# GLA gates beside the values in 512 columns, and results turned by VectorE and by stores

## The chip, the core and the metric

The kernel runs on one core of one Trainium2 chip (the other cores idle). The metric is the time of one execution on the device in microseconds (us); of several runs the median is given. Everything is fp32 on the outside; the large products run in fp32r, split in two parts.

## What is computed

One step of a hybrid decoder layer, for a prompt of 2048 tokens and for 8 samples that each add one token to a state. The width is 1024. Cut to what matters:

```
hn  = rmsnorm(x) * (1 + scale) + shift           # shift, scale, gate = silu(c) @ w_ada + b_ada
xa, za, q, k, v, glr, zg = split(hn @ w_in)      # 1024, 1024, 512, 512, 1024, 16, 1024 columns

# RG-LRU group: 8 blocks of 128 channels
xc    = conv4(xa);  gx, ga = sigmoid(xc @ w_gate + b)
h     = scan(a(ga) * h + sqrt(1 - a^2) * gx * xc);   y_lru = h * silu(za)

# GLA group: 4 heads, keys of 128, values of 256
S_t   = diag(alpha_t) S_(t-1) + k_t^T v_t;  o_t = q_t S_t
y_gla = o * rsqrt(mean(o*o) + eps) * g_gla_norm * silu(zg)

y     = rmsnorm(x + gate * (concat(y_lru, y_gla) @ w_out))
```

The last states of the convolution, of the LRU and of GLA, for the prompt and for the samples, are outputs too.

## The kernel before

**Products.** Each factor is split into a high and a low part, and a product is three matmuls: high by high, high by low, low by high. The normalized input stands in `hh` and `hl`, feature by token. The prompt goes in two halves of 1024 tokens (`TH`); a half is cut in segments (`SEGS`): 512 and 512 in half 0; 384, 384 and 264 in half 1, where the last holds 256 tokens and the 8 samples. TensorE's accumulators are four PSUM banks (`acc`, L53), two banks for transposes (`tps`, L56), one for the state update (`kv`) and one for the GLA output (`o`).

**Weights.** `weights` (L261) brings a piece of `w_in`. In half 0 the raw piece (512 KB) is loaded, split by ACT (L281) and VectorE (L282), and the parts (1 MB) are stored (L301); in half 1 the parts are loaded back (L284). The split weights have three buffers, the raw ones two. SyncE (SP) issues all loads and most stores in order.

**Projections.** `project` (L615) holds weights still and streams a segment's tokens (L621 to L623): the result is channel by token. It gives XA, ZA, K, Q and the GLA gates ZG. `values` (L734) streams weights past a 128-token tile instead (`value_mm`, L314, L317 to L319, 24 matmuls of 256 columns a tile): token by channel, as GLA wants its values. In half 1 `sample_values` (L710) gives the 8 samples' values with raw fp32 weights (L718), in four column groups side by side.

**Order.** The program is written in TensorE's order. `after(units, fn)` (L645) puts a step on a heap by a clock that `tick` (L649) advances with each unit of projection; so the work of GLA chunks, LRU gates and outputs is put between projections. Each head is followed by LRU tiles: heads in the order 3, 0, 1, 2 (`HEADS`), LRU tiles (0), (1, 2), (3, 4), (5, 6, 7) behind them (`LRU_TILES`), in each half. `ada_gate` (L665) computes the final gate from `w_ada` in four steps that each load 1 MB, under the first LRU tile.

**A GLA head** (`gla_head`, L937): values; keys and queries by segment with their decays (`gla_decay`, `gla_qk`); then, chunk by chunk of 128 tokens, state and output (`gla_chunk`, L847; L856 to L864 on TensorE, S updated at L865 and L866, the output copied to `on` at L869, its squares summed by ACT at L148). `gla_norm` (L872) takes the rsqrt (twelve small VectorE instructions, L125) and scales `on` by it (L877). The head's gates are projected channel by token, 128 channels at a time, and `silu2` (L915) forms z(1 + tanh(z/2)) with ACT (L919) and VectorE (L920). `gla_out` (L923) turns `on` by TensorE transposes (L929; in the last segment a small matmul, L931, puts the samples behind), multiplies by g_gla_norm (`gsc`) and the gate on VectorE (L934), and `spill` (L630) stores 128 channels by the segment's tokens to `mixd` in DRAM by ACT's queue (L635). The samples' state and output are `sample_state` (L879) and `sample_out` (L897).

**An LRU tile** (`lru_units`, L1010): XA by segment, convolution on VectorE (L1027), gate matmuls in three parts (L1053 to L1055), and a chain of ACT and VectorE over the whole half (L1056 to L1068: multiplications, square root, scan), then ZA with its silu, and the product (L1084), spilled as above.

**Tail.** `load_mix` (L1202) loads 128 tokens of all 16 channel tiles from `mixd` and splits them; `split_wo` (L1233) splits w_out; `mm3` (L1325) does the output projection, `Out` the gate, the residual and the last norm. It begins under the last LRU tiles of half 1.

## Time and profile before

| what | value |
|---|---|
| median of 3 runs | 1497.78 us (1495.71 to 1497.83) |
| the profiled execution | 1496.99 us |
| its span, first to last instruction | 1495.2 us |
| TensorE busy | 1474.0 us, 8973 matmul records |
| VectorE busy | 846.1 us, 2139 instructions |
| ACT busy | 594.7 us, 1058 instructions |
| granted TensorE clock, mean | 0.997 |

The span is what the trace covers; 1.8 us of the execution lie around it. PE is TensorE, PEld its weight loads (which overlap the matmuls), DVE is VectorE, POOL GpSimd, SP SyncE. A row of a grouped view names line, engine, operation, output<-inputs, shape, count, then busy us and mean ns of one, then the engine's idle time just before and what ended it. Matmuls are pipelined, so that the length of one is longer than its distance from the next.

### The profile page before, as it was taken

The numbers are of one execution on the slowest core, as the hardware profiler recorded it, in microseconds if no ns is written. First come the engines' busy times: TensorE is split into PE (matmuls) and PEld (weight loads), VectorE is DVE, ScalarE is ACT, GpSimd is POOL, SyncE is SP. The second block draws the span as 40 slices with busy tenths as digits, with TensorE's granted clock in tenths as the row PEclk, the third lists the DMA queues.
The fourth block names the chain that finished last, engine by engine and source line by source line (L and its number), as shares of the span: only waits on it lengthen the run. The fifth ranks groups of instructions, "written<-read, shape, count | busy, mean of one in ns | idle before, by whom it ended". The sixth has DMA issues, their size and how long they took to land.

```text
span 1495.2 us, 22861 instructions
## 1 busy us (share of the span) xinstructions
PE 1474.0 (99%) x8973; PEld 1306.9 (87%) x8973; DVE 846.1 (57%) x2139; ACT 594.7 (40%) x1058; POOL 92.9 (6%) x117
## 2 busy tenths in 40 slices
...
GB/s 324 256 152 169 222 124 166 158 161 107 165 152 139 219 122 127 141 117 149 141 110 113 163 96 134 132 83 168 179 99 229 171 113 85 113 111 64 108 43 29
DMA packets 141681, 211.30 MB, mean 141 GB/s; under 512 B 7427, under 2 KB 102563, under 8 KB 140926
## 3 DMA queue, kind: packets, MB, share of 16 engines
...
q10 hardware_dynamic: 32048, 16.00, 3.6%
...
## 4 chain that ended last, share of the span: by engine, by line
PE 52%; DVE 2%; ACT 2%; DMA 1%; issue 0%; POOL 0%; ACTq 0%; DVEq 0%
PE acc L1328 7%; PE acc L1329 7%; PE acc L1330 7%; PE acc L621 7%; PE acc L622 7%; PE acc L623 7%; PE acc L317 1%; PE acc L318 1%; PE acc L319 1%; PE po L864 1%; PE tp L929 1%; PE tp L830 0%; DMA raw<-in_w_out_dram 0%; PE acc L1053 0%; DMA w<-parts 0%
## 5 line engine op out<-in xcount | busy, mean ns | idle before, releaser
L621 PE MATMUL acc<-hh,w 128*128 128x384 f32 (+2 forms) x1256 | 445.7, 355 | 0.5 <-DMA w<-parts 0.4
L622 PE MATMUL acc<-hl,w 128*128 128x384 f32 (+2 forms) x1256 | 435.5, 347 | 0.0
L623 PE MATMUL acc<-hh,w 128*128 128x384 f32 (+2 forms) x1256 | 434.0, 346 | 0.0
L621 PEld LDWEIGHTS acc<-hh,w 128*128 128x128 f32 x1256 | 236.0, 188 | 23.1 <-issue 3.2
L623 PEld LDWEIGHTS acc<-hh,w 128*128 128x128 f32 x1256 | 235.9, 188 | 19.6
L622 PEld LDWEIGHTS acc<-hl,w 128*128 128x128 f32 x1256 | 236.1, 188 | 19.3 <-issue 0.4
L1329 PE MATMUL acc<-wol,mh 128*128 128x512 f32 (+1 forms) x528 | 202.3, 383 | 1.3 <-DVE wol L1236 1.3
L1328 PE MATMUL acc<-woh,mh 128*128 128x512 f32 (+1 forms) x528 | 203.0, 384 | 0.0
L1330 PE MATMUL acc<-woh,ml 128*128 128x512 f32 (+1 forms) x528 | 202.1, 383 | 0.0
L317 PE MATMUL acc<-w,hh 128*128 128x256 f32 (+1 forms) x508 | 145.1, 286 | 0.3 <-POOL hh L182 0.2
L319 PE MATMUL acc<-w,hl 128*128 128x256 f32 (+1 forms) x508 | 143.5, 282 | 0.2 <-DVE hl L206 0.2
L318 PE MATMUL acc<-w,hh 128*128 128x256 f32 (+1 forms) x508 | 143.2, 282 | 0.0
L1351 DVE TENSOR_TENSOR r<-acc,gbc 128x512 f32<-128x512 f32 (+1 forms) x33 | 22.3, 675 | 190.1 <-PE acc L1330 179.5
L1328 PEld LDWEIGHTS acc<-woh,mh 128*128 128x128 f32 x528 | 99.2, 188 | 26.1 <-issue 6.9
L1329 PEld LDWEIGHTS acc<-wol,mh 128*128 128x128 f32 x528 | 99.2, 188 | 21.1 <-DVE wol L1236 2.2
L1330 PEld LDWEIGHTS acc<-woh,ml 128*128 128x128 f32 x528 | 99.2, 188 | 19.4
L919 ACT ACTIVATE zs<-acc 128x512 f32<-128x512 f32 (+2 forms) x80 | 41.1, 513 | 179.5 <-PE acc L623 179.4
L920 DVE SCALAR_TENSOR_TENSOR zs<-zs,acc 128x512 f32<-128x512 f32 (+2 forms) x80 | 46.3, 578 | 91.3 <-ACT zs L919 91.3
L317 PEld LDWEIGHTS acc<-w,hh 128*128 128x128 f32 x508 | 96.1, 189 | 2.1 <-DVE vl L748 0.4
L319 PEld LDWEIGHTS acc<-w,hl 128*128 128x128 f32 x508 | 96.0, 189 | 0.4 <-DVE hl L206 0.4
L318 PEld LDWEIGHTS acc<-w,hh 128*128 128x128 f32 x508 | 95.5, 188 | 0.2
L1027 DVE SCALAR_TENSOR_TENSOR cv<-xa,vecT,cv 128x384 f32<-128x384 f32 (+2 forms) x120 | 76.9, 650 | 29.8 <-POOL cv L1025 29.5
...
## 6 DMA issues: line engine op xcount, KB each, us to landing
...
```

Source lines behind the costliest of these rows:

```text
L317: PE.matmul(ps, hh[:, kt, c], hi[:, kt % 4], start=kt == 0, stop=False)
L318: PE.matmul(ps, hh[:, kt, c], lo[:, kt % 4], start=False, stop=False)
L319: PE.matmul(ps, hl[:, kt, c], hi[:, kt % 4], start=False, stop=kt == KT - 1)
L621: PE.matmul(ps[:, :n], hi[:, kt], a, start=kt == 0, stop=False)
L622: PE.matmul(ps[:, :n], hi[:, kt], b, start=False, stop=False)
L623: PE.matmul(ps[:, :n], lo[:, kt], a, start=False, stop=kt == KT - 1)
L919: S.activation(z, ps, AF.Tanh, scale=0.5)
L920: V.scalar_tensor_tensor(z, z, 1.0, ps, op0=OP.add, op1=OP.mult)
L1027: V.scalar_tensor_tensor(cv[:, cq], xa[:, cq.start + k:cq.stop + k], cw[k], cv[:, cq], op0=OP.mult, op1=OP.add)
L1328: PE.matmul(ps, mh[:, q], woh[k][:, c], start=first, stop=False)
L1329: PE.matmul(ps, mh[:, q], wol[k][:, c], start=False, stop=False)
L1330: PE.matmul(ps, ml[:, q], woh[k][:, c], start=False, stop=last)
```

## The change

- For heads 0, 1 and 2, in each half, a new class `Pairs` projects the values and the gates together, token by channel: 256 columns of V and 256 of ZG side by side, 512 to a matmul, four 128-token tiles at a time in the four `acc` banks. `group(0)` (tiles 0 to 3) stands before the last LRU tile of the head before, `group(1)` (tiles 4 to 7) after it. The weights come in four quarters of two k-tiles (1 MB of parts each): the first has a buffer of its own, the other three take the three buffers, and are loaded for each group. The weights of K and Q are asked for inside group 1, Q's after step (2, 3), the last but one of its 16.
- While a group runs, the LRU gate matmuls use the transpose banks. Before `group(0)`, what is left of `ada_gate` is emitted (`flush_kind(4)`); `ada_gate` begins inside the first head, and its steps follow each other after 1.5 units instead of 3.
- Head 3 keeps `values`; its gates are projected token by channel as well, eight tiles with 256 columns.
- The gates' silu is formed per 128-token tile (`gate_out`), stored to DRAM (`zd`) and brought back a segment at a time into one buffer `zl` (`gate_back`).
- `gla_norm` only forms rs. `gla_out` multiplies `on` by rs and the gate, turns each 32x32 block on VectorE into `zl`, and four stores a segment (ACT's queue) put the blocks where they belong in `yd`, in runs of 32 elements. `g_gla_norm` is folded into the split of w_out. A segment's chunks after the first wait, in emission, for `gla_out` of the segment before.
- The samples' gates come with their values in half 1: four sample parts in each `group(0)` (raw fp32 weights, 128 columns in each of four column groups, through a transpose bank, added up in `zr` by VectorE), for head 3 in `sample_gates`; `turn_gates` turns them by small matmuls; `gla_out_samples` writes the samples' results. `sample_out` uses a transpose bank instead of `o`.
- In the tail `load_mix` loads a token tile in six pieces instead of four.

Counted in the two programs, TensorE's matmuls are: of 512 columns token by channel 0 before and 1152 after, of 256 columns (V) 1152 and 384; of `project`, 512 wide 1464 and 1080, 384 wide 1536 and 1152, 264 wide 768 and 576; transposes of `on` 128 and 0; sample matmuls of 64 columns 96 and 0, of 128 columns 0 and 112; eight small ones for the samples' gates are new.

```diff
+LAST = (6, 7)
...
-    mixd = dpool.tile([16, P, 16, P], F32, tag="mixd", name="mixd")
+    mixd = dpool.tile([16, P, 8, P], F32, tag="mixd", name="mixd")
+    yd = dpool.tile([H, 16, 2, P, P], F32, tag="yd", name="yd")
+    zd = dpool.tile([H, 16, P, DV], F32, tag="zd", name="zd")
...
+    def flush_kind(n):
+        while any(e[n] for e in pend):
+            e = min(e for e in pend if e[n])
             pend.remove(e)
             heapq.heapify(pend)
+            clock[0] = max(clock[0], e[0])
             e[2]()
+
+    def flush_gla():
+        flush_kind(3)
...
-            after(3, mm)
+            after(1.5, mm, bank=True)
...
     def gla_norm(nch, run):
-        _, on, ss = run
-        rs = gp.tile([P, 4], F32, tag="ors", name="ors")
+        ss = run[2]
+        rs = gp.tile([P, 4], F32, tag="ors", name="ors", bufs=2)
         rsqrt(gp, rs[:, :nch], ss[:, :nch], nch, P, 1.0 / DV)
-        for c in range(nch):
-            V.tensor_scalar(on[:, c], on[:, c], rs[:, c:c + 1], None, op0=OP.mult)
+        return rs
...
-        po = psum.tile([P, 512], F32, tag="o", name="po", bufs=1)[:, :DV]
+        po = tps()[:, :DV]
...
-    def gla_out(half, h, s, on, os_, zs):
+    gated_rows, back, side_by_side = set(), [None], [False]
+    def gate_out(h, tt, ps, z):
+        S.activation(z, ps, AF.Tanh, scale=0.5)
+        V.scalar_tensor_tensor(z, z, 1.0, ps, op0=OP.add, op1=OP.mult)
+    def gate_store(half, h, tt, z):
+        t = half * 8 + tt
+        S.dma_start(zd[h, t:t + 2].rearrange("t p c -> p t c"), z.rearrange("p (t c) -> p t c", c=DV))
+        gated_rows.update((h, t + n) for n in range(2))
+    def gate_back(half, h, s):
         c0, n = SEGS[half][s]
-        nch = min(n, TH - c0) // P
-        for dt in range(2):
-            pt = tps()
-            for c in range(nch):
-                PE.transpose(pt[:, c * P:(c + 1) * P], on[:, c, dt * P:(dt + 1) * P], ident)
-            if os_ is not None:
-                PE.matmul(pt[:, nch * P:n], os_[:, dt * P:(dt + 1) * P], sel4, start=True, stop=True)
-            ct = 2 * h + dt
-            z = zs[dt]
-            V.scalar_tensor_tensor(z, pt[:, :n], gsc[:, ct:ct + 1], z, op0=OP.mult, op1=OP.mult)
-            spill(z, 8 + ct, half, c0, n)
-
-    def gla_head(half, h, wv=None):
+        t0, nch = half * 8 + c0 // P, min(n, TH - c0) // P
+        if back[0] or any((h, t) not in gated_rows for t in range(t0, t0 + nch)):
+            return None
+        back[0] = h, half, s
+        z = yp.tile([P, 4, DV], F32, tag="zl", name="zl")
+        SP.dma_start(z[:, :nch], zd[h, t0:t0 + nch].rearrange("t p c -> p t c"))
+        return z
+    def pair_raw(h, q):
+        raw = wp.tile([P, 1088], F32, tag="wr", name="wr")[:, :1024].rearrange("p (k n) -> p k n", n=512)
+        for n, col in enumerate((V0 + h * DV, ZG + h * DV)):
+            SP.dma_start(raw[:, :, n * DV:(n + 1) * DV], i["w_in"][
+                0, 2 * q * P:(2 * q + 2) * P, col:col + DV].rearrange("(k p) n -> p k n", p=P))
+        return raw
+    def pair_weights(h, q):
+        both = (yp.tile([P, 2, 1088], F32R, tag="wy", name="w") if q == 0 else
+                wp.tile([P, 2, 1088], F32R, tag="w", name="w", bufs=3))
+        c = slice(48, 48 + 1024)
+        hi, lo = [both[:, j, c].rearrange("p (k n) -> p k n", n=512) for j in range(2)]
+        if ("vz", h, q) in parts:
+            SP.dma_start(both[:, :, c].bitcast(F32), parts["vz", h, q])
+            return hi, lo
+        raw = pair_raw(h, q)
+        S.copy(hi, raw)
+        V.tensor_tensor(lo, raw, hi.bitcast(F32), op=OP.subtract)
+        parts["vz", h, q] = dpool.tile([P, 2, 1024], F32, tag=f"vz{h}_{q}", name="parts")
+        SP.dma_start(parts["vz", h, q], both[:, :, c].bitcast(F32))
+        return hi, lo
+    class Pairs:
+        def __init__(self, half, h):
+            self.half, self.h, self.w, self.zs = half, h, [None], []
+            self.v, self.wkq = ([], []), []
+        def group(self, g):
+            half, h, w = self.half, self.h, self.w
+            if g == 0:
+                flush_kind(4)
+            w[1:] = [pair_weights(h, q) for q in range(1, 4)]
+            for x, tag in zip(self.v, ("vh", "vl")):
+                x.append(gp.tile([P, 4, DV], F32R, tag=tag, name=tag, bufs=2))
+            vh, vl = [x[g] for x in self.v]
+            side_by_side[0] = True
+            ps = [acc() for _ in range(4)]
+            samples = g == 0 and half == 1
+            raws = [pair_raw(h, q) for q in range(2)] if samples else []
+            for q, j in [(q, j) for q in (0, 1) for j in range(4)] + [(q, j) for j in range(4) for q in (2, 3)]:
+                hi, lo = w[q]
+                tt = 4 * g + j
+                c = slice(tt * P, (tt + 1) * P)
+                for k in range(2):
+                    kt = 2 * q + k
+                    PE.matmul(ps[j], hh[:, kt, c], hi[:, k], start=kt == 0, stop=False)
+                    PE.matmul(ps[j], hh[:, kt, c], lo[:, k], start=False, stop=False)
+                    PE.matmul(ps[j], hl[:, kt, c], hi[:, k], start=False, stop=kt == KT - 1)
+                if q == 3:
+                    S.copy(vh[:, j], ps[j][:, :DV])
+                    V.tensor_tensor(vl[:, j], ps[j][:, :DV], vh[:, j].bitcast(F32), op=OP.subtract)
+                    if j % 2 == 0:
+                        z = lp.tile([P, 512], F32, tag="zs", name="zs", bufs=4)
+                    gate_out(h, tt, ps[j][:, DV:], z[:, j % 2 * DV:(j % 2 + 1) * DV])
+                    if j % 2:
+                        after(0.25, lambda tt=tt, z=z: gate_store(half, h, tt - 1, z), True)
+                tick(0.25)
+                if g == 1 and (q, j) in ((1, 3), (2, 3)):
+                    self.wkq.append(weights((0, K0, Q0)[q] + h * DK, DK))
+                if samples and (q, j) in ((0, 3), (1, 3), (2, 0), (3, 1)):
+                    sample_part(q, raws[q])
+                    if q < 2:
+                        raws.append(pair_raw(h, q + 2))
+            side_by_side[0] = False
+            if samples:
+                for n in range(2):
+                    SP.dma_start(vsd[h][:, n * P:(n + 1) * P], zr[32 * n:32 * n + NS])
+                after(1, lambda: turn_gates([ident[:, 64 + 32 * n:64 + 32 * n + NS] for n in range(2)], self.zs), True)
+    def sample_part(q, raw):
+        ps = tps()[:, :P]
+        for k in range(2):
+            for g in range(4):
+                PE.matmul(ps[32 * g:32 * g + NS], fs[:, 2 * q + k], raw[:, k, g * P:(g + 1) * P],
+                          start=k == 0, stop=k == 1)
+        for g in range(4):
+            r = slice(32 * g, 32 * g + NS)
+            if q == 0:
+                (S.copy if g % 2 else V.tensor_copy)(zr[r], ps[r])
+            else:
+                V.tensor_tensor(zr[r], zr[r], ps[r], op=OP.add)
+    def turn_gates(sels, zs):
+        pt = tps()[:, :2 * NS]
+        for n in range(2):
+            PE.matmul(pt[:, n * NS:(n + 1) * NS], zr, sels[n], start=True, stop=True)
+        z = yp.tile([P, 2 * NS], F32, tag="zq", name="zq")
+        S.activation(z, pt, AF.Tanh, scale=0.5)
+        V.scalar_tensor_tensor(z, z, 1.0, pt, op0=OP.add, op1=OP.mult)
+        zs.append(z)
+    def sample_gates(w, zs):
+        ps = acc()[:, :P]
+        for m in range(0, KT, 2):
+            for g in range(4):
+                kt = m + g // 2
+                c = g % 2 * P
+                PE.matmul(ps[32 * g:32 * g + NS], fs[:, kt], w[kt // 4][2][:, kt % 4, c:c + P],
+                          start=m == 0, stop=m == KT - 2)
+        for g in range(4):
+            r = slice(32 * g, 32 * g + NS)
+            (S.copy if g % 2 else V.tensor_copy)(zr[r], ps[r])
+        after(1, lambda: turn_gates([sel2[:, n] for n in range(2)], zs), True)
+    def gla_out(half, h, s, on, rs, z):
+        t0, nch = SEGS[half][s][0] // P, min(SEGS[half][s][1], TH - SEGS[half][s][0]) // P
+        for c in range(nch):
+            V.scalar_tensor_tensor(on[:, c], on[:, c], rs[:, c:c + 1], z[:, c], op0=OP.mult, op1=OP.mult)
+        for c in range(nch):
+            V.transpose(z[:, c], on[:, c])
+        def store():
+            back[0] = None
+            y = z[:, :nch].rearrange("p c (a i) -> p (c a) i", i=32)
+            for b in range(4):
+                S.dma_start(dram(yd, (h * 16 + half * 8 + t0) * 2 * P * P + 32 * b,
+                                 [[P, 32], [32 * P, nch * 8], [1, 32]]), y[32 * b:32 * b + 32])
+        after(1, store, True)
+    def gla_out_samples(h, os_, z):
+        pt = tps()[:, :2 * NS]
+        for n in range(2):
+            PE.matmul(pt[:, n * NS:(n + 1) * NS], os_[:, n * P:(n + 1) * P], sel4, start=True, stop=True)
+        for n in range(2):
+            ct = 2 * h + n
+            c = slice(n * NS, (n + 1) * NS)
+            V.scalar_tensor_tensor(mixs[:, 8 + ct], pt[:, c], gsc[:, ct:ct + 1], z[:, c], op0=OP.mult, op1=OP.mult)
...
+            if c == 1:
+                if rows_busy[0]:
+                    after(0.5, lambda: chunks(s, c), True)
+                    return
+                rows_busy[0] = True
+            if c == 2:
+                zl[s] = gate_back(half, h, s)
...
-        wz = [weights(ZG + (2 * h + dt) * P, P) for dt in range(2)]
-        for s in range(ns):
-            c0, n = SEGS[half][s]
-            for dt in range(2):
-                zs[s, dt] = silu2(wz[dt], c0, n)
-                tick()
+            ada_gate()
+        if pairs:
+            return
+        wz = row_weights(ZG + h * DV, DV, half == 1)
+        if half == 1:
+            sample_gates(wz, sgs)
+        for tt in range(8):
+            if tt % 2 == 0:
+                z = lp.tile([P, 512], F32, tag="zs", name="zs", bufs=4)
+            ps = acc()[:, :DV]
+            value_mm(ps, slice(tt * P, (tt + 1) * P), wz, DV, (0, KT))
+            gate_out(h, tt, ps, z[:, tt % 2 * DV:(tt % 2 + 1) * DV])
+            if tt % 2:
+                after(0.5, lambda tt=tt, z=z: gate_store(half, h, tt - 1, z), True)
+            tick(0.75 if half else 0.5)
...
+                    ps = (tps() if side_by_side[0] else acc())[:, :sn]
...
+                after(2 if half == 0 and j in (0, 5, 6) else 3, lambda: gates(t, [s]))
...
+    for half in range(2):
+        pairs = None
+        for k, h in enumerate(HEADS):
+            gla_head(half, h, None if half or k else wv0, pairs)
+            js = LRU_TILES[k]
+            if k == 3:
+                lru(1, js[:-len(LAST)]) if half else lru_last_a(js)
+                break
+            pairs = Pairs(half, HEADS[k + 1])
+            pairs.w[0] = pair_weights(HEADS[k + 1], 0)
+            lru(half, js[:-1])
+            pairs.group(0)
+            lru(half, js[-1:])
+            pairs.group(1)
     flush_gla()
+    ypx.close()
...
+                dst, k = mr[-1][:, p[0][0] - q:p[0][0] - q + n], p[0][1]
+                if k < 8:
+                    (G if tt < 2 and k in LAST else SP).dma_start(dst, mixd[tt, :, k:k + n])
+                else:
+                    SP.dma_start(dst, yd[(k - 8) // 2, tt, k % 2:k % 2 + n].rearrange("k p t -> p k t"))
...
+            g = gsc[:, k - 8:k - 7]
+            S.activation(woh[k], raws[k], AF.Copy, scale=g)
+            V.scalar_tensor_tensor(wol[k], raws[k], g, woh[k].bitcast(F32), op0=OP.mult, op1=OP.subtract)
```

87 lines of the change are left out of this document (44 added, 43 removed).

## The prediction

> **What bounds the kernel now.** I read the page first: its span, the busy times, the chain that ended last.
>
> ```profile
> span 1495.2 us, 22861 instructions
> PE 1474.0 (99%) x8973; PEld 1306.9 (87%) x8973; DVE 846.1 (57%) x2139; ACT 594.7 (40%) x1058; POOL 92.9 (6%) x117
> ...
> PE 52%; DVE 2%; ACT 2%; DMA 1%; issue 0%; POOL 0%; ACTq 0%; DVEq 0%
> ```
>
> TensorE is busy 99% of the span, and where the chain is named it is TensorE's by far. The profiled execution took 1496.99 us, 1.8 us more than its span and 0.8 under the median of the runs shown (1497.78). I forecast against 1496.99.
>
> The table by stage tells whether this holds where the change works. Four of its rows, from the second half of the prompt:
>
> ```profile
> 600.00:700.00 100.00, 99.46 (x740) 96.61 (x739) 63.16 (x206) 40.09 (x81) 6.15 (x11) 1.00 0.43 139
> 700.00:800.00 100.00, 99.87 (x690) 97.23 (x690) 58.28 (x201) 35.78 (x77) 6.44 (x11) 1.00 0.36 121
> 800.00:900.00 100.00, 99.48 (x745) 97.45 (x744) 55.78 (x152) 44.39 (x79) 7.43 (x7) 1.00 0.39 127
> 900.00:1000.00 100.00, 100.00 (x757) 98.47 (x757) 60.38 (x172) 43.14 (x78) 7.37 (x10) 1.00 0.38 128
> ```
>
> Columns: stretch, its length, then PE, PEld, DVE, ACT, POOL busy (instructions), granted clock, DMA share, GB/s. The clock is 1.00, VectorE has some 40% free on average, the DMA engines 60%. So TensorE's own time is what counts, and any new wait of TensorE adds whole.
>
> A matmul's printed duration is no price, since matmuls overlap. The pace is, from start to start over undisturbed runs. Four stretches of TensorE's timeline give it, by first row and first row after:
>
> ```profile
> 257.12 0.39 PE L621 MATMUL acc<-hh,w 128*128 128x512 f32 x1
> ...
> 273.44 0.39 PE L1053 MATMUL acc<-xh,wg 128*128 128x512 f32 x1
> ...
> 281.60 0.28 PE L317 MATMUL acc<-w,hh 128*128 128x256 f32 x1
> ...
> 304.21 0.40 PE L761 MATMUL acc<-gls,g2s 128*128 128x512 f32 x1
> ...
> 931.97 0.28 PE L621 MATMUL acc<-hh,w 128*128 128x264 f32 x1
> ...
> 935.57 0.34 PE L621 MATMUL acc<-hh,w 128*128 128x384 f32 x1
> ...
> 946.78 0.33 PE L621 MATMUL acc<-hh,w 128*128 128x384 f32 x1
> ...
> 957.18 0.28 PE L621 MATMUL acc<-hh,w 128*128 128x264 f32 x1
> ```
>
> They hold 72, 192, 30 and 60 matmuls, so one of 512 columns takes 16.32/72 = 0.2267 us, of 256 22.61/192 = 0.1178, of 264 3.60/30 = 0.1200, of 384 10.40/60 = 0.1733. Two rows of the page matter too (busy us, mean ns of one | idle before it, and what ended that):
>
> ```profile
> L317 PE MATMUL acc<-w,hh 128*128 128x256 f32 (+1 forms) x508 | 145.1, 286 | 0.3 <-POOL hh L182 0.2
> ...
> L317 PEld LDWEIGHTS acc<-w,hh 128*128 128x128 f32 x508 | 96.1, 189 | 2.1 <-DVE vl L748 0.4
> ```
>
> A weight load lasts 189 ns, yet matmuls 117.8 ns apart follow without gaps: loads overlap, and a 256-wide matmul isn't bound by them.
>
> **The change part by part.** *Pairing* (heads 0, 1, 2). In half 0 a head's values are 192 matmuls of 256 and its gates 96 of 512: 192 x 0.1178 + 96 x 0.2267 = 44.4 us. In half 1 the gates are 96 of 384 and 48 of 264: 22.6 + 16.6 + 5.8 = 45.0. Paired, both are 192 of 512 = 43.5 us. That is -0.85 and -1.5 a head, three heads: -7.0. Head 3's gates turn from 96 x 512 (21.8) and 96 x 384 + 48 x 264 (22.4) into 192 x 256 (22.6) each: +1.0. Together **-6.0 us**. The evictions stay off the path; they split one 512-wide pair into two 256-wide.
>
> The Trainium skill, "TensorE: Matmul & The Clock Gate", section "Wait — 56ns, not 53.3ns?", has a warm gap of N/2.4 ns + 2.5: 109 ns for 256 and 216 for 512. The trace's 117.8 and 226.7 differ; by the rule the pairing, worked out the same way, would give -2.1 instead of -6.0, and the forecast below would be 3.9 us later. The measurement decides.
>
> *Turning* the results by TensorE goes: 128 transposes. The chain shows six of them, a grouped row the count, and the line's own view what it waited for:
>
> ```profile
> 669.24 0.66 PE tp L929 x6
> ```
> ```profile
> L929 PE MATMUL tp<-ident,on 128*128 128x128 f32 x128 | 19.0, 277 | 0.0
> ```
> ```profile
>   DVE on L877: 0.7, 3
>   issue: 0.2, 1
> ```
>
> 128 x 0.66/6 = **-14.1 us**, and 0.9 us of waits: **-0.9**. What replaces it stands on VectorE, ACT's queue and the DMA engines, off the path as long as TensorE never waits for it; the results are read back only in the tail, hundreds of us later for the early heads.
>
> *Samples.* The gates of the 8 samples no longer ride in the 264-wide matmuls; they come with the values, in fp32, 128 columns by four. 24 sets of four at 64 columns go, 28 sets at 128 come. The nearest rows, from the chain and from the timeline:
>
> ```profile
> 689.01 1.01 PE acc L718 x64
> ```
> ```profile
> 137.88 1.07 PE L677 MATMUL acc<-xt,sc 128*32 128x256 f32 x16
> 138.88 0.50 PE L1053 MATMUL acc<-xh,wg 128*128 128x512 f32 x1
> ```
>
> One set leaves eight records: 64 columns cost 1.01/8 = 0.126 us, 256 columns 1.00/2 = 0.50. For 128 I take the value in proportion, 0.25: 28 x 0.25 - 24 x 0.126 = **+4.0 us** (+0.5 if it cost no more than 64 columns, +11 if as much as 256). Eight small matmuls turn these gates; the similar L931 lasts 216 ns:
>
> ```profile
> L931 PE MATMUL tp<-sel,os 128*128 128x8 f32 x16 | 2.3, 216 | 0.0
> ```
>
> Between nothing and 8 x 0.216 = 1.7 I take half, **+0.9**. TensorE's own work: -6.0 - 14.1 - 0.9 + 4.0 + 0.9 = **-16.1 us**.
>
> **New waits.** (a) A group holds all four banks that projections use, so LRU gates and samples go through the two transpose banks, each of which VectorE or ACT must empty first. In half 1 the four sample parts of group(0) add sixteen small evictions. VectorE's queue then holds, ahead of them, the LRU tile's chain:
>
> ```profile
> L869 DVE COPY on<-po 128x256 f32<-128x256 f32 x64 | 26.7, 417 | 0.0
> ...
> L748 DVE TENSOR_TENSOR vl<-acc,vh 128x256 fp32r<-128x256 f32 x56 | 23.6, 421 | 53.1 <-ACT vh L747 52.9
> ...
> L877 DVE TENSOR_SCALAR on<-on,ors 128x256 f32<-128x256 f32 x64 | 18.6, 350 | 0.6
> ...
> L1068 DVE TENSOR_TENSOR_SCAN tg<-xl,hc,tx 128x1024 f32<-128x1024 f32 x6 | 14.3, 2384 | 0.0
> ...
> L1064 DVE SCALAR_TENSOR_TENSOR tx<-tx,cv 128x1032 f32<-128x1032 f32 x8 | 9.9, 1233 | 6.7 <-ACT tx L1056 6.6
> ...
> L1066 DVE TENSOR_TENSOR tx<-tx,tg 128x1032 f32<-128x1032 f32 x8 | 9.8, 1226 | 0.0
> ...
> L1084 DVE SCALAR_TENSOR_TENSOR zs<-tg,zs 128x384 f32<-128x384 f32 x16 | 8.7, 549 | 0.0
> ...
> L1065 DVE SCALAR_TENSOR_TENSOR tg<-xl,tg 128x1032 f32<-128x1032 f32 x6 | 7.4, 1233 | 18.3 <-ACT tg L1063 18.3
> ...
> L1084 DVE SCALAR_TENSOR_TENSOR zs<-tg,zs 128x264 f32<-128x264 f32 x8 | 3.4, 426 | 0.1
> ```
>
> The chain, L1064 to L1084, is 1.23 + 1.23 + 1.23 + 2.38 + 0.55 + 0.55 + 0.43 = 7.6 us. Also in a sample group of about 24 us (21.8 of matmuls, 2 of samples) come four evictions of values and gates (8 x 0.42 = 3.4), chunk work (two chunks of three passes, some 2.4), three multiplications by rs and gate (1.3), three block transposes (unseen; between L877's 0.35 and twice that, 1.1 to 2.1), the rsqrt's small steps and the sample additions (some 24 at 0.15 to 0.2, about 4). Together 20 to 21 us of 24: VectorE goes from 60% to over 80%, and what is queued behind the chain comes late. TensorE waits for nothing at best, for the whole 7.6 us a head at worst. Since two banks give slack, I take a fifth, 1.5 us a head, three heads: **+4.5** (0 to 22.8).
>
> (b) ada_gate's matmuls move under the first group, and each step issues two 512 KB loads for the next. One step follows its predecessor by some 20 matmuls of 512, 4.6 us. A load of the same 1 MB is in the chain:
>
> ```profile
> 846.67 5.97 DMA w<-parts
> ```
>
> 5.97 - 4.6 = 1.4 us late; I take **+1.0** (0 to 4.2, three such steps).
>
> (c) The Q weights are asked for behind 15 of group 1's 16 steps, 15 x 6 x 0.2267 = 20.4 us in. K's first segment is done at 21.8 + 24 x 0.1733 = 25.9 us. 5.5 us for a load of 5.97: 0.5 us late, three heads, **+1.5** (0 to 3). The value weights of the groups have 12 us and more. In half 0 K's segment is wider, and nothing is late.
>
> Sum of waits +7.0; -16.1 + 7.0 = -9.1: 1496.99 - 9.1 = **1487.9, say 1488 us**.
>
> **The rivals.**
> 1. *No new wait*: the queues have slack, as the averages by stage (56 to 63% of VectorE) say. 1496.99 - 16.1 = 1481. Against it: the averages hide a chain of 7.6 us in one piece. Chance 0.20.
> 2. *Slower: VectorE's queue in the sample groups*. TensorE waits for a sample's bank while the LRU chain runs, in three groups. From 13.6/3 = 4.5 us a head on (16.1 less the 2.5 of b and c) the gain is gone; with the whole chain, 22.8 + 2.5 - 16.1 = +9.2: 1506. For it: 20 of 24 us filled, and evictions whose order the program fixes. Against it: two banks, and chains that need not start right there. Chance 0.17.
> 3. *Stores in 128-byte pieces*. The turned results leave in 32-element runs, 2 M elements / 32 = 65,536 pieces. The nearest row is ACT's queue before, in 512-byte packets:
>
> ```profile
> q10 hardware_dynamic: 32048, 16.00, 3.6%
> ```
>
> 3.6% of 16 x 1495.2 us over 32048 is 27 ns a packet. At that price the pieces take 65,536/16 x 27 ns = 110 us of each engine, 0.07 of the span on top of 0.36 to 0.43: room enough. But a segment of three chunks leaves in four stores of 32 x 24 pieces; these 3072 take 3072/16 x 27 ns = 5.2 us of all 16 engines, and where they meet the Q load, they stretch it. With half of that in each head of half 1 it is 3.1 us late instead of 0.5, three heads +9.3: waits of 14.8, 1495.7, no change. Chance 0.12, with other sums of small waits of that size. The Trainium skill, "DMA: Bandwidth & Descriptors", section "Specifications", speaks for this one: under 512 B a transfer misses line rate, since the engine reads, modifies and writes. No run here shows such pieces; were each twice as long, the share would rise by 0.15, and the Q load would be 5.7 us late.
> 4. *Pairing saves much*: by printed durations, 192 x (2 x 281 - 389) ns would be 33 us for each half-head. The paces refute it. Chance 0.01.
>
> That the change doesn't do what it says, I rule out for TensorE's count: the transposes are gone from its program, 1152 matmuls of 512 columns stand for the pairs.
>
> **How the numbers follow.** Forecast 1488 (1484 to 1493, with waits between 3 and 12 us): 0.50. Rival 1: 0.20; rival 2: 0.17; rival 3: 0.12; rival 4: 0.01. The bound for "same" is 0.2%, 3 us, about what a measurement of this kernel can tell: faster is under 1494.8. So faster 0.50 + 0.20 + 0.01 = 0.71, same 0.12, slower 0.17. Unknown sizes: samples +0.5 to +11 (-3.5 to +7 on the sum), waits 0 to 30. The range leaves out the upper part of rival 2 and rival 4: 1480 to 1500.
>
> **What the profile after would show.** The paired lines at a pace of 227 ns and no L929's like; sample sets at 0.25 us; under TensorE's waits, DVE's evictions of the sample banks at three places in half 1, of 1 to 2 us each, ahead of all others; the Q load under 1 us each. I am wrong if fp32 sets of 128 columns cost 0.5 us, if the block transposes take over 0.7 us each, or if the projections' four banks make TensorE wait between groups, in half 0 too, for the evictions of the group before.

## The result, and the profile after

| | median | runs | ratio to before, 95% interval |
|---|---|---|---|
| before | 1497.80 us (1495.71 to 1497.87) | 4 | |
| changed | 1510.68 us (1507.84 to 1511.32) | 4 | 1.0086 [1.0068, 1.0103] |

The change makes the kernel 12.9 us slower. 1488 was forecast, with 1480 to 1500 as the range: it is outside, and on the other side of no change.

The page of the changed kernel, the same three lines as before:

```profile
span 1509.0 us, 21924 instructions
...
PE 1475.7 (98%) x8317; PEld 1267.1 (84%) x8317; DVE 870.1 (58%) x2230; ACT 599.4 (40%) x1088; POOL 80.3 (5%) x117
...
PE 49%; DVE 6%; ACT 3%; issue 2%; DMA 1%; POOL 1%; ACTq 0%; DVEq 0%; POOLq 0%
```

656 matmul records are gone, yet TensorE's busy time is 1.7 us higher and the span 13.8 us longer; in the chain that ended last, VectorE has risen from 2% to 6%. The table by stage shows two different things. First the four stretches that the prediction shows, then two others, and those two in the kernel before:

```profile
600.00:700.00 100.00, 98.57 (x734) 89.50 (x733) 58.55 (x194) 33.17 (x74) 4.92 (x9) 1.00 0.58 185
700.00:800.00 100.00, 99.86 (x605) 94.07 (x604) 61.77 (x183) 42.65 (x85) 7.84 (x13) 1.00 0.51 158
800.00:900.00 100.00, 99.80 (x598) 88.47 (x597) 58.76 (x169) 42.13 (x77) 2.49 (x3) 1.00 0.56 178
900.00:1000.00 100.00, 99.67 (x650) 90.62 (x650) 65.97 (x210) 37.80 (x79) 8.47 (x14) 1.00 0.56 176
...
500.00:600.00 100.00, 93.04 (x551) 78.94 (x550) 73.90 (x177) 59.20 (x101) 16.79 (x20) 0.97 0.50 158
1100.00:1200.00 100.00, 92.86 (x482) 71.17 (x482) 64.31 (x105) 53.32 (x73) 8.88 (x11) 0.98 0.52 162
```
```profile
500.00:600.00 100.00, 98.39 (x612) 84.94 (x611) 74.00 (x164) 61.57 (x101) 18.46 (x21) 1.00 0.45 147
1100.00:1200.00 100.00, 97.65 (x491) 75.37 (x490) 64.55 (x108) 46.09 (x68) 6.33 (x8) 1.00 0.49 160
```

In the middle of half 1, where the groups with samples stand, TensorE is as full as before: the wait that the forecast feared most, and rival 2's, isn't there. Where half 0 ends (500 to 600) and where half 1 runs out (1100 to 1200), TensorE loses about 5 us of 100 each that it did not lose before, and its clock falls.

The pace of the paired matmuls: first row of a group, the next, and the first row behind its 96.

```profile
721.27 0.40 PE L1014 MATMUL acc<-w,hh 128*128 128x512 f32 x1
721.51 0.40 PE L1015 MATMUL acc<-w,hh 128*128 128x512 f32 x1
...
743.66 0.34 PE L779 MATMUL acc<-gls,g2s 128*128 128x384 f32 x1
```

22.39 us / 96 = 0.2332 us, not 0.2267. The new waits of TensorE, the five longest (us in total, times, longest):

```profile
PE tp L183 <- ACT hnf L186: 3.0, 3, 2.1
PE acc L1247 <- ACT xh L1234: 2.9, 2, 2.7
PE acc L1247 <- DVE zs L937: 2.5, 1, 2.5
PE acc L695 <- DMA xt<-in_w_ada_dram: 2.2, 1, 2.2
PE acc L1247 <- ACT xa L1312: 2.1, 1, 2.1
```

L183 is `modulate`, the transposes of the next half's input at the end of half 0; L1247 is the first of the LRU gate matmuls; L695 is `ada_gate`. All but L695's are LRU work and the half's end, and none of these was foretold at its place; `ada_gate`'s wait was.

**Where the 13.8 us came from.** I added up the distances from one matmul's start to the next by the program's function, so that a wait counts to the matmul before it. In us, before, after and difference:

| function | before | after | |
|---|---|---|---|
| pairs (`group`), `project`, `value_mm` | 906.8 | 908.4 | +1.6 |
| `gla_out`, and `gla_out_samples` behind it | 15.0 | 2.2 | -12.8 |
| samples' values and gates (`sample_part`, `sample_gates`, the 64-column sets) | 3.0 | 7.6 | +4.6 |
| `turn_gates` | 0 | 1.5 | +1.5 |
| `modulate` | 5.9 | 11.1 | +5.2 |
| `gla_chunk` | 64.8 | 68.8 | +4.1 |
| LRU `gates` | 47.8 | 51.6 | +3.8 |
| `state_outputs` | 0.9 | 3.8 | +2.9 |
| `sample_values`, its 68-column matmuls | 1.4 | 4.2 | +2.8 |
| all others | | | 0.0 |

The first four lines are TensorE's own work: -5.1 against a forecast of -16.1. The rest, +18.9 against +7.0, is waits and the slower clock behind some of them (the 2.2 us of L695 stand under `gla_chunk`); by the page, TensorE's idle time alone rose by 12.1 us, from 21.2 to 33.3 of the span. The two differences, 11.0 and 11.9, are the miss of 22.9.

**The stall at 530 us, step by step.** It is the longest. The timelines of ACT and then VectorE in the changed kernel (start, length, instruction, and in brackets the idle time before it and what ended that):

```profile
514.07 1.06 ACT L1257 ACTIVATE tg<-tg 128x1024 f32<-128x1024 f32 x1
```
```profile
511.35 0.34 DVE L884 TENSOR_SCALAR S<-S,f 128x256 f32<-128x256 f32 x1
517.32 0.42 DVE L883 TENSOR_TENSOR S<-S,pkv 128x256 f32<-128x256 f32 x1 [5.62 <-PE po L882]
...
523.96 0.42 DVE L883 TENSOR_TENSOR S<-S,pkv 128x256 f32<-128x256 f32 x1 [5.63 <-PE po L882]
...
524.96 1.21 DVE L1259 SCALAR_TENSOR_TENSOR tg<-xl,tg 128x1024 f32<-128x1024 f32 x1
...
528.00 2.28 DVE L1262 TENSOR_TENSOR_SCAN tg<-xl,tx 128x1024 f32<-128x1024 f32 x1
```

VectorE idles 5.6 us twice, each time until TensorE reaches a GLA chunk whose state it must update (L883). L1259, the next step of the LRU chain, multiplies what ACT's L1257 had ready at 515.13. It runs at 524.96, since it stands behind both chunks in VectorE's queue, and for 7.8 of these 9.8 us VectorE does nothing (515.13 to 517.32, and 5.63). So the scan runs from 528.0, most of the next tile's convolution behind it, and TensorE, which needs that convolution, stops:

```profile
529.25 1.04 PE L183 MATMUL tp<-ident,xt 128*128 128x128 f32 x8
532.96 1.22 PE L1247 MATMUL acc<-xh,wg 128*128 128x512 f32 x2 [2.68 <-ACT xh L1234]
533.98 0.63 PE L633 MATMUL acc<-hh,w 128*128 128x512 f32 x1
534.41 0.63 PE L634 MATMUL acc<-hl,w 128*128 128x512 f32 x1
...
536.35 0.40 PE L1248 MATMUL acc<-xl,wg 128*128 128x512 f32 x1
536.59 0.40 PE L1249 MATMUL acc<-xh,wg 128*128 128x512 f32 x1
```

Two things are to be seen: 2.68 us of idle time, and behind it matmuls of 512 columns 0.43 us apart (533.98 to 534.41) until 536.1, then 0.24. The granted clock says the same, as the eighth column:

```profile
530.00:535.00 5.00, 2.32 (x8) 1.72 (x7) 5.00 (x12) 0.66 (x2) 0.00 (x0) 0.77 0.35 105
535.00:540.00 5.00, 5.00 (x21) 4.04 (x20) 4.68 (x10) 1.79 (x3) 0.00 (x0) 0.89 0.28 114
```

The clock was halved for some 3.2 us of work, which costs 1.6 beside the stall. It fell like that behind the waits at 530, 567 and 1100 us, and not behind those at 125 and 1122. So 4 to 5 of the 18.9 us are clock.

Why only three of the five? The clock's records change on a fixed grid of 3.41 us. The waits at 530, 567 and 1100 put 2.42, 2.36 and 2.16 us of idle time into one such window, and the window after it ran at half the clock; those at 125 and 1122 lie across a border, with 1.15 and 1.06, and 1.13 and 1.35 us. In the traces of all twenty kernels, from 40 us on, each of the 58 windows at full clock with 1.85 us of idle time or more was followed by one at half, none of the 8438 with less than 1.67 was, and of the ten between four were.

**The other stalls.** The one at 1100 is of the same kind. VectorE's queue stands before the product by the gates, which are still on their way back from DRAM (`zl`), and the steps of the next tile's convolution behind it wait too:

```profile
1098.48 0.88 DVE L1083 SCALAR_TENSOR_TENSOR on<-on,ors,zl 128x256 f32<-128x256 f32 x2 [2.09 <-DMA zl<-zd]
...
1099.96 0.52 DVE L1235 TENSOR_TENSOR xl<-cv,xh 128x384 fp32r<-128x384 f32 x1
```

L1235's input was ready at 1096.47 (ACT's L1234). The convolution ends late, ACT's cast of it stands ahead of the copy that frees TensorE's bank (L1312, at 1102.75), and TensorE waits until 1103.28. Ahead of the stall at 1122, though, VectorE is busy for 16.1 of the 17 us from 1108 to 1125; load isn't ruled out there. That at 567 was not followed back to its start.

### The profile page after: what moved, and what is told of

Read it like the earlier page. It is cut to its first block, busy times and chain, and to the rows that moved or that the text cites. A ratio compares the mean times of both kernels' runs of the same rounds, so it can differ in the third digit from the quotient of the medians.

```text
span 1509.0 us, 21924 instructions
## 1 busy us (share of the span) xinstructions
PE 1475.7 (98%) x8317; PEld 1267.1 (84%) x8317; DVE 870.1 (58%) x2230; ACT 599.4 (40%) x1088; POOL 80.3 (5%) x117
## 3 DMA queue, kind: packets, MB, share of 16 engines
q10 hardware_dynamic: 90544, 24.39, 6.9%
q8 instruction: 65, 1.06, 0.3%
## 4 chain that ended last, share of the span: by engine, by line
PE 49%; DVE 6%; ACT 3%; issue 2%; DMA 1%; POOL 1%; ACTq 0%; DVEq 0%; POOLq 0%
PE acc L1537 7%; PE acc L1538 7%; PE acc L1539 7%; PE acc L633 4%; PE acc L635 4%; PE acc L634 4%; PE acc L1014 3%; PE acc L1016 2%; PE acc L1015 2%; PE acc L325 1%; PE acc L327 1%; PE acc L326 1%; DVE tg L1262 1%; PE po L882 1%; DMA mr<-mixd 1%
## 5 line engine op out<-in xcount | busy, mean ns | idle before, releaser
L633 PE MATMUL acc<-hh,w 128*128 128x384 f32 (+2 forms) x936 | 330.7, 353 | 0.2 <-ACT tg L1250 0.2
L634 PE MATMUL acc<-hl,w 128*128 128x384 f32 (+2 forms) x936 | 323.8, 346 | 0.0
L635 PE MATMUL acc<-hh,w 128*128 128x384 f32 (+2 forms) x936 | 323.6, 346 | 0.0
L634 PEld LDWEIGHTS acc<-hl,w 128*128 128x128 f32 x936 | 176.1, 188 | 15.5 <-issue 0.9
L633 PEld LDWEIGHTS acc<-hh,w 128*128 128x128 f32 x936 | 176.1, 188 | 15.1 <-ACT tg L1250 0.4
L635 PEld LDWEIGHTS acc<-hh,w 128*128 128x128 f32 x936 | 175.9, 188 | 14.6
L1014 PE MATMUL acc<-w,hh 128*128 128x512 f32 x384 | 155.4, 405 | 0.0
L1016 PE MATMUL acc<-w,hl 128*128 128x512 f32 x384 | 151.7, 395 | 0.0
L1015 PE MATMUL acc<-w,hh 128*128 128x512 f32 x384 | 151.6, 395 | 0.0
L1221 DVE SCALAR_TENSOR_TENSOR cv<-xa,vecT,cv 128x512 f32<-128x512 f32 (+2 forms) x120 | 77.1, 644 | 23.1 <-POOL cv L1219 22.1
L1014 PEld LDWEIGHTS acc<-w,hh 128*128 128x128 f32 x384 | 72.1, 188 | 19.4 <-issue 3.2
L1015 PEld LDWEIGHTS acc<-w,hh 128*128 128x128 f32 x384 | 72.1, 188 | 16.4
L1418 ACT CAST mh<-mr 128x256 fp32r<-128x256 f32 (+2 forms) x48 | 34.8, 759 | 111.6 <-PE acc L1538 106.2
L325 PE MATMUL acc<-w,hh 128*128 128x256 f32 (+1 forms) x252 | 73.4, 291 | 0.1
```

What stands on the lines that cost most here:

```text
L325: PE.matmul(ps, hh[:, kt, c], hi[:, kt % 4], start=kt == 0, stop=False)
L633: PE.matmul(ps[:, :n], hi[:, kt], a, start=kt == 0, stop=False)
L634: PE.matmul(ps[:, :n], hi[:, kt], b, start=False, stop=False)
L635: PE.matmul(ps[:, :n], lo[:, kt], a, start=False, stop=kt == KT - 1)
L1014: PE.matmul(ps[j], hh[:, kt, c], hi[:, k], start=kt == 0, stop=False)
L1015: PE.matmul(ps[j], hh[:, kt, c], lo[:, k], start=False, stop=False)
```

## The experiments

Theories at the outset: **(1)** the pace of 512-wide matmuls depends on the byte place of the streamed weights, and the pairs' weights stand at an unfavourable one; **(2)** the stalls at the ends of the halves come since the last head's gates were moved ahead, so that less projection stands over its chunks and the last LRU chains. Rivals: the pace is the pairs' own, and VectorE's added work (multiplying and turning) makes the stalls. Theories that came up later are told by the expectations themselves. Each run's time is beside a before of 1496.8 to 1497.7 us on the same chip.

**The pace.** The weights of each head and half at another offset; then all of them at good ones.

```diff
-        c = slice(48, 48 + 1024)
+        off = 16 if q == 0 else 0        # e5; e1: another for each head and half
+        c = slice(off, off + 1024)
```

> Each head's and half's paired weights stand at another place in their buffers, so that the moving operand lies 0, 32, 64, 96, 128 or 224 bytes off the stationary activations within 256 bytes (192 and 128 in the changed kernel). Theory 1 (the pace hangs on where the two operands stand to each other): the paired matmuls of head 0 in half 0, at the same place, go at 226.7 ns, the others at 233.3; that is 192 x 6.6 ns = 1.3 us, so the time is 1507 to 1511. Rival (with the activations stationary and weights moving, 512 columns always take 233.3): all six runs of matmuls at 233.3 ns, no difference between heads.

1508.77 us, one run. Undisturbed pace by the place that the edit gives the weights' first byte, in bytes from the start of their buffer (the first quarter, in a buffer of its own, 64 bytes further): 226.8 ns at 0, 229.2 at 64, 232.5 at 128, and 233.2 to 233.4 at 32, 96, 224 and (the changed kernel) 192. Theory 1 holds.

> The changed kernel with the paired weights put at the place within 256 bytes where the activations stand (offset 0, and 16 elements in the first quarter's own buffer). Theory 1, as the run with several offsets showed it: all paired matmuls at 226.7 ns instead of 233.3, 1152 x 6.6 ns = -7.6 us: 1501 to 1505. Rival (the stalls at the halves' ends take the gain back, since VectorE sets the end there): 1507 to 1511.

1506.35 us, 1.0063 [1.0050, 1.0075]: 4.3 us under the changed kernel. The pairs fell from 273.4 to 268.7 us. One run of 48 matmuls in it:

```profile
176.51 0.39 PE L1015 MATMUL acc<-w,hh 128*128 128x512 f32 x1
...
187.39 0.39 PE L1015 MATMUL acc<-w,hh 128*128 128x512 f32 x1
```

10.88/48 = 0.2267. So the pace that I forecast was to be had, but over all 1152 it is 268.7/1152 = 0.2332 us even here: other work breaks in at 41 places, mostly for 0.1 to 0.2 us each, 6.3 us in all (4.9 at 37 places in the changed kernel), and some stretches run at 230 to 235 ns, 1.3 us. So of the 7.5 us that the place costs in the changed kernel, 1152 x 6.5 ns, 4.7 came back.

Does the place matter in the kernel before, at 256 columns?

```diff
-        q = 48 if n == DV else 0
+        q = 0                            # e12; e13: another for each head and half
```

> The kernel before the change, with the value weights (256 columns) at offset 0 instead of 48 elements, so that they stand where the activations stand within 256 bytes. Theory 1 for 256 columns too: all of them at 113.3 ns rather than mostly 117.8, 1152 x 3.7 ns = -4 us: 1492 to 1495. Rival (the rule holds for 512 columns alone): 117 to 120 ns, 1496 to 1500.

1500.63 us, 1.0026 [1.0016, 1.0035], slower: at 0 a matmul of 256 takes 119.8 to 120.0 ns in all six stretches of heads 0, 1 and 2. At 192 bytes, in the kernel before, heads 1 and 2 have 117.8, but head 0 114.6 in half 0 and 113.4 in half 1:

```profile
690.29 0.28 PE L319 MATMUL acc<-w,hl 128*128 128x256 f32 x1
...
711.83 0.34 PE L761 MATMUL acc<-gls,g2s 128*128 128x384 f32 x1
```

190 matmuls in 21.54 us are 113.4 ns each.

> The kernel before the change, value weights of heads 0, 1, 2 at offsets 8, 16, 24 elements in half 0 and 32, 40, 56 in half 1 (32, 64, 96, 128, 160, 224 bytes; 192 before). Known so far for 256 columns: 120.0 ns at 0 bytes, 117.8 or 113.3 at 192. Theory 1a (the pace is set by the place, differently for each width): the six stretches differ from each other and some place gives a steady 113.3. Rival (at 256 columns it is how a stretch begins, not the place): every stretch is at 113.3, 117.8 or 120.0 without order. The time is 1493 to 1501 either way.

1500.52 us, one run; in the mean of a stretch 117.0 ns at 32 bytes, 117.8 at 64, 120.0 at 96, 117.3 to 118.7 at 128, 160 and 224. So the place matters here too, and 0, the best for 512 columns, is among the slowest for 256. But it doesn't set the pace alone, since 192 gave two. I have no rule for it.

**Pairing and turning apart.** First the groups left out, the rest as changed (e2), or left out ahead of the last head alone (e3):

```diff
-            pairs = Pairs(half, HEADS[k + 1])
-            pairs.w[0] = pair_weights(HEADS[k + 1], 0)
-            lru(half, js[:-1])
-            pairs.group(0)
-            lru(half, js[-1:])
-            pairs.group(1)
+            lru(half, js)
```

> No head is paired: values, then keys and queries, then gates in eight tiles of 256 columns, for all four heads as for head 3; the turning by VectorE and stores stays. Theory 2 (TensorE's stalls at the end of each half come from the last head's gates having been moved ahead, so that 22 us less of projections stand over its chunks and the last LRU chains): these stalls go; what stays is -15.0 for the transposes, +4 for the samples' gates, +2.6 for turning them, +4.2 for gates of 256 columns: about 1493 (1489 to 1498). Rival (VectorE's turning of the results delays the chains and makes the stalls): the stalls of about 15 us stay, 1504 to 1509.

1536.73 us, 1.0264 [1.0249, 1.0280]. Both forecasts missed; the waits say why:

```profile
PE acc L325 <- ACT tx L1250: 20.9, 2, 10.5
PE acc L1248 <- DVE xl L1235: 7.9, 3, 4.9
```

Twice TensorE waits over 10 us for an accumulator bank. Two LRU gate products hold banks; ACT is to empty them into `tx` (L1250), of which there is one buffer, still in use by the chain of the tile before. In half 0 the gates of the tiles 1 to 4 come 3 units after their tile in the changed order, where it was 2, which suits groups between tiles and nothing else. So this run measures a clash of the order, not the pairs.

> Heads 0 and 1 stay paired, the last head (2) has values and gates apart as head 3 has, its gates behind its keys and queries. Theory 2: the stalls at the ends of both halves (about 15 us with the slow clock behind them) go, those of the pace (two thirds of 7.6 us) stay: 1494 to 1500. Rival: the stalls are still there: 1506 to 1511.

1523.21 us, 1.0172 [1.0155, 1.0189]: the same clash once, 11.6 us at 416, though `modulate` lost its 5.2. It tells nothing more.

To have the turning alone without that clash, e6 leaves the pairs out and restores the order of before (gates after 2 units in half 0, but for the last tile, and `ada_gate` after 3):

> The turning alone: no head paired, gates token by channel behind keys and queries, results turned by VectorE and stores; the order of gates, of the flush and of ada_gate as in the kernel before. Theory 3 (stalls come where VectorE's turning and the last chains meet with little projection work over them; with the old order there is enough): -15.0 transposes, +7.5 samples and their turning, +4.2 gates of 256 columns, stalls under 4 us: 1491 to 1498. Rival (the turning on VectorE costs TensorE its stalls in any order): 1501 or more.

1511.93 us, 1.0098 [1.0084, 1.0112], in the rival's range. The transposes' 15.0 us are saved, and 30 come back: `gates` +11.3, `gla_chunk` +5.1, `sample_gates` +4.0, `state_outputs` +2.5, the rest in small terms. The largest wait:

```profile
PE acc L1247 <- DVE xl L1234: 8.3, 3, 4.9
```

At 515 us ACT's queue stands on the copy of the next tile's XA, for which TensorE's projection isn't done, ahead of the chain of the tile before (L1255, which then runs at 519.0); VectorE idles for 5.4 us meanwhile. This part alone costs as much as the whole change.

e14 is the reverse: pairs (aligned, with e10's edit below), and the results turned by TensorE again.

> Pairing alone: the aligned kernel with the early flush (1504.5), but the results are turned by TensorE's transposes again (128 of them, 14 us) and copied by VectorE, stored in rows of 512 bytes. Theory 5 (VectorE's order and the lost cover make the stalls, not the turning itself): 14 us more of TensorE's work, VectorE's transposes (24 us in all) replaced by copies of about as much: 1513 to 1520. Rival (block transposes and 128-byte stores make the stalls): the stalls of about 12 us go with them, 1504 to 1509.

1517.11 us, 1.0137 [1.0120, 1.0153]: `gla_out` is back with 13.7 us, `project` costs 7.7 more, at its steps into other work, and `modulate`, `gates` and `state_outputs` give back 9.5, all against e10. The time is as Theory 5 had it, but a good part of the stalls went with the block transposes, as its rival had it. Pairs alone gain nothing either.

**The stalls at the ends: VectorE's work?** e4 leaves out head 2's multiplication by rs and gate, and its block transposes (that head's prompt results are not formed).

> As the changed kernel, but for head 2 the multiplication by rs and gate and the block transposes on VectorE are left out (its results are not computed; the stores still go). Theory 2: the stalls at the ends of the halves stay, over three quarters of them, 1505 to 1511. Rival (VectorE's turning makes them): they go, under 1500.

1505.47 us, one run. The stalls at the ends fell by 13.5 us, as the rival had it, but other waits came (`project` +4.1, `decay` +1.4, `group` +1.2), and the net was -5.2, so that the time is at the edge of Theory 2's range. It doesn't tell less work from another order, since VectorE's queue changed as well: the chain now stands ahead of both later chunks.

```profile
519.99 1.22 DVE L1259 SCALAR_TENSOR_TENSOR tg<-xl,tg 128x1024 f32<-128x1024 f32 x1 [3.03 <-ACT tg L1257]
...
529.07 0.41 DVE L883 TENSOR_TENSOR S<-S,pkv 128x256 f32<-128x256 f32 x1
```

In e8 head 2's product goes to ACT and GpSimd instead (aligned kernel):

> Aligned, all three heads paired; for head 2 the product by rs and gate goes from VectorE (0.44 us each, 16 of them) to ACT and GpSimd; the block transposes stay on VectorE. Theory 3 (VectorE's queue is what is late at the halves' ends): the stalls fall by about half, 1495 to 1500. Rival (ACT is as late as VectorE, or only the missing projections count): 1501 to 1506.

1510.07 us, 1.0083 [1.0069, 1.0096]. Both forecasts missed: 3.7 us slower than e5, the stalls unchanged, though 16 x 0.44 = 7 us of work are off VectorE. The order is e5's here (the chain stands behind the second chunk), and ACT and GpSimd have more to do. So that part of VectorE's load doesn't set the stalls; that its added work plays no part isn't shown.

**The stalls at the ends: order?** Four edits of the order, all on the aligned kernel: the last head's pairs left out and the GLA outputs earlier (e7), the LRU gates later (e9), the GLA outputs of the half's last head emitted ahead of the last tile's units (e10), and the last two together, with `ada_gate`'s steps half a unit later (e11). e7 also has the gates of the tiles (3, 4) sooner.

```diff
-                after(2 if half == 0 and j in (0, 5, 6) else 3, lambda: gates(t, [s]))
+                after(2 if half == 0 and j == 0 else 3, lambda: gates(t, [s]))            # e9, e11
...
+        flush_gla()                                                                       # e10, e11
+        xt += [hn_load(1), hn_load(2)]
         for s in range(2):
-            if s == 0:
-                flush_gla()
-                xt += [hn_load(1), hn_load(2)]
```

> Aligned pairs for heads 0 and 1, head 2 with values and gates apart; LRU gates before head 2 after 2 units and the flush at its old place, so that the stalls of 11.8 and 5.1 us that the run with the last head apart had (banks held by late LRU gates) should not come. Theory 3: no stalls at the ends, -7.6 for the pace, -13 for the stalls: 1488 to 1496. Rival: the stalls stay, 1500 or more.

1514.83 us, 1.0110 [1.0095, 1.0126]; in the rival's range, but not for its reason: waits of 4.9 us at 537, 3.6 at 402 and 2.4 at 451 stand in place of those removed. With the last head apart, here and in e3, `modulate` loses its 5.2 us, but the orders that came with it bring other waits, so Theory 2 stays open.

> Aligned kernel; in half 0 the gate matmuls of LRU tiles 5 and 6 stand after 3 units instead of 2. Theory 4 (no engine lacks throughput at the end of half 0; TensorE reaches the gate matmuls before the convolution, which stands in VectorE's queue behind the chain of the tile before and chunk steps that wait for TensorE): the stall at 530 us (2.8, and some 1.4 at half the clock behind it) goes: 1501 to 1504 where the aligned kernel has 1506.4. Rival (VectorE has too much to do there): the wait turns up at the next step, 1505 to 1508.

1524.65 us, 1.0178 [1.0163, 1.0194]; missed. The stall at 530 went, and two of another kind came, e2's:

```profile
PE acc L633 <- ACT tx L1251: 12.1, 1, 12.1
PE acc L325 <- ACT tx L1251: 10.3, 1, 10.3
```

> Aligned kernel; the flush of the last head and the loads of half 1's tokens at their place of before, ahead of the last LRU tile of half 0 rather than after its first unit. Theory 4: the modulation of half 1's tokens starts 11 us earlier and the waits at 565 to 590 us (+5.2 in modulate, +2.8 in the sample values) go: 1497 to 1501. Rival (VectorE has too much to do there): they move forward, 1504 to 1508.

1504.47 us, 1.0047 [1.0030, 1.0063]: 1.9 us under e5, a fifth to a third of what was expected; `sample_values` -3.2 and `modulate` -1.6, but `gates` +2.8 and `value_mm` +2.2.

> Both of these, and ada_gate's steps after 2 units instead of 1.5 (its loads then have 6 us and more). Theory 4: the gains add, less 1 to 2 us for w_ada's wait too: 1493 to 1498, no slower than the kernel before. Rival: 1503 to 1508.

1530.77 us, 1.0223 [1.0208, 1.0239]: e9's clash again, in three places of 8 to 10 us.

**The stores.** The turned results leave in long rows of the block transposes' buffer, that is in other places of `yd`, so that the tail then reads results out of place; bytes and number of stores are the same.

```diff
-                S.dma_start(dram(yd, (h * 16 + half * 8 + t0) * 2 * P * P + 32 * b,
-                                 [[P, 32], [32 * P, nch * 8], [1, 32]]), y[32 * b:32 * b + 32])
+                S.dma_start(dram(yd, (h * 16 + half * 8 + t0) * 2 * P * P + 32 * b * nch * DV,
+                                 [[nch * DV, 32], [1, nch * DV]]), z[32 * b:32 * b + 32, :nch])
```

> The aligned kernel with the early flush (1504.5), with the turned results stored in long rows of 1 KB and more instead of 32-element pieces (they land in the wrong places, so the prompt's output is not the reference's). Theory 5: no wait of TensorE hangs on these stores, 1503 to 1506. Rival (65,536 pieces of 128 bytes hold up loads, or ACT behind them): 3 us or more less, under 1501.

1497.97 us, 1.0007 [0.9995, 1.0018]: 6.5 us under e10. That looked like the price of 65,536 pieces of 128 bytes. But the build orders each engine's queue itself: this edit changes only where the stores write, and yet in the trace 83 of ACT's 1235 instructions and 127 of VectorE's 2230 stand in another order. So the edit was made in two more kernels, the changed one (e16) and the turning alone (e17), and a third run (e18) keeps the pieces and moves the order a little:

```diff
-        after(1, store, True)
+        after(1.5, store, True)          # e18, on e10
```

> The changed kernel with one edit: the turned results leave in long rows (and land in other places). Theory A, the 128-byte pieces themselves cost time wherever they stand: 6 to 7 us less than the changed kernel, as in the aligned one, so 1503 to 1506 us. Theory B, the earlier gain was the order that the build gives the queues of ACT, VectorE and TensorE, which changes with the stores: any sign, over 3 us away from 1504, with the stalls at the ends of the halves in other places.

1503.23 us, 1.0040 [1.0028, 1.0052]: 7.5 under the changed kernel, in Theory A's range.

> The kernel with the turning alone (no pairs), its stores in long rows. Theory A: 6 to 7 us under 1511.9, so 1504 to 1507 us. Theory B: away from that by over 3 us, on either side.

1497.92 us, 1.0002 [0.9994, 1.0011]: 14 under e6. By Theory A the pieces should have given half of it.

> The aligned kernel with the early outputs of GLA, its stores in 128-byte pieces asked for half a unit of projection later, nothing else changed; the queues' order changes with it (about 30% of ACT's rows). Theory A, pieces: within 2 us of 1504.5. Theory B, order: over 3 us away from it.

1500.84 us, 1.0024 [1.0015, 1.0032]: 3.6 under e10, with every piece as it was. So the order, with the half unit that the stores come later, can be worth that much; the two ratios' intervals just overlap (e10's ends at 1.0030), and the trace is of this kernel's fastest execution (1498.28, where the eleven reach 1504.12). Its VectorE at the stall of above:

```profile
513.45 0.42 DVE L883 TENSOR_TENSOR S<-S,pkv 128x256 f32<-128x256 f32 x1 [5.62 <-PE po L882]
...
515.70 1.22 DVE L1260 SCALAR_TENSOR_TENSOR tg<-xl,tg 128x1024 f32<-128x1024 f32 x1
...
518.75 2.29 DVE L1263 TENSOR_TENSOR_SCAN tg<-xl,tx 128x1024 f32<-128x1024 f32 x1
...
520.96 0.40 DVE L883 TENSOR_TENSOR S<-S,pkv 128x256 f32<-128x256 f32 x1
```

L1260 is the changed kernel's L1259. It runs ahead of the second chunk's L883, where it had run behind it, 2.3 us after the first chunk's instead of 7.6 us; the convolution of the next tile is early as well, and TensorE doesn't stop there. The same in e15 and e16, whose stores are long: L1259 starts 0.9 us after the first chunk's L883.

```profile
519.47 0.42 DVE L883 TENSOR_TENSOR S<-S,pkv 128x256 f32<-128x256 f32 x1 [5.62 <-PE po L882]
520.40 1.22 DVE L1259 SCALAR_TENSOR_TENSOR tg<-xl,tg 128x1024 f32<-128x1024 f32 x1
```

(e16's timeline.) And e10, which stalls at 530 for 2.67 us, has it behind the second, like the changed kernel:

```profile
516.00 0.42 DVE L883 TENSOR_TENSOR S<-S,pkv 128x256 f32<-128x256 f32 x1 [5.62 <-PE po L882]
522.64 0.42 DVE L883 TENSOR_TENSOR S<-S,pkv 128x256 f32<-128x256 f32 x1 [5.63 <-PE po L882]
523.64 1.20 DVE L1260 SCALAR_TENSOR_TENSOR tg<-xl,tg 128x1024 f32<-128x1024 f32 x1
```

So with this stall, at least, one place in VectorE's queue decides: of the eight kernels with the chain behind the first chunk's L883, the changed one, e1, e5, e8 and e10 have it behind the second too and stall for 2.67 or 2.68 us, and e15, e16 and e18 have it ahead of the second and don't. In e4 and e14 it stands ahead of both; there TensorE waits 1.56 us for a chunk's state instead. It also takes the clock along: in e15, e16 and e18 the granted clock from 500 to 600 us is 1.00 again. How much of the long rows' 6.5 to 14 us is the pieces and how much the order stays open; no run held the order fixed and changed the pieces.

None of the kernels beats the one before; of those that put every result in its place, e18 comes nearest, at 3.2 us above it.

## Why the prediction was wrong, point by point

- **TensorE sets the time; any new wait of it adds whole**: right, before and after.
- **Pairing -6.0**: mis-sized. It measured +1.6. The pace of 0.2267 us was taken from `project`, whose weights stand still and whose tokens stream; the pairs stream weights at a place 192 bytes into their buffer, and ran at 0.2332 (e1, e5). That is 1152 x 6.5 ns = 7.5 us; short breaks by other work cost the pairs 4.8 more, 273.4 us in all where 1152 x 0.2267 is 261.2. Against that, the projections that went had such breaks too and freed 6.2 us more than by their paces; and the value matmuls that went freed 1.5 less, since the 117.8 ns were read from head 1 and head 0's ran at 113.4 to 114.6. 7.5 + 4.8 - 6.2 + 1.5 = 7.6, the miss of this term. The Trainium skill's N/2.4 + 2.5 ns ("TensorE: Matmul & The Clock Gate", "Wait — 56ns, not 53.3ns?") has no term for the place; its 216 ns for 512 columns was the pace of no undisturbed stretch here, the fastest being 226.7.
- **Transposes -14.1 and -0.9**: `gla_out`'s 15.0 us went, as said. But 1.1 us of them were the samples' small matmuls, and those cost 2.2 in their new form, which I had left out: -12.8 in all.
- **Samples +4.0**: right, +4.6. Sets of 128 columns took 6.6/24 = 0.28 us, near the 0.25 chosen. **Turning of gates +0.9**: +1.5, near the upper end of 1.7.
- **(a) Sample groups +4.5**: the wait didn't come. Its matmuls in the changed kernel:

```profile
L1044 PE MATMUL tp<-wr,fs 128*8 128x128 f32 x192 | 7.5, 273 | 0.4 <-ACT zr L1049 0.4
```

 0.4 us of idle time in all of half 1. Two banks were slack enough. **(b) `ada_gate` +1.0**: 2.2, in one wait, within its bounds. **(c) Q weights +1.5**: none.
- **"Off the path"**: this is the step that failed. What replaced the transposes, I said, costs nothing as long as TensorE never waits for it. I then asked that question at the groups only, not at the ends of the halves, where the last head's outputs, the last LRU chains and the next half's input meet in VectorE's and ACT's queues. 14.7 us of waits came there (`modulate`, `gates`, `state_outputs`, `sample_values`), clock included, where I had put nothing. VectorE's average hides it: 73.90% busy from 500 to 600 us, and 74.00% before. At 530 it isn't load but the place in the queue: VectorE idled 7.8 us with the path's next step ready behind a step that waited for TensorE. At 1100 the step ahead waited for the gates from DRAM. For the rest of the 14.7 us the steps aren't shown, and whether VectorE's added work makes part of them stays open (e4, e14 and the full queue before 1122 speak for it, e8 against). Also I took the order of the queues to be the program's; the build changes it, so that an edit far off moves a chain by one chunk.
- **Block transposes 0.35 to 0.7 us each**: at the lower end.

```profile
L1085 DVE STREAM_TRANSPOSE zl<-on 128x256 f32<-128x256 f32 x64 | 24.4, 419 | 0.0
```

- **Rival 2**, slower by VectorE's queue, had the sign, the kind and nearly the price (1506 against 1510.7), but not the place: a chain held up by other work, not other work by a chain, and at the ends.
- **Rival 3**, the pieces: the Q load was never late. The room that it worked out was there, since the queue with all pieces takes less than feared:

```profile
q10 hardware_dynamic: 90544, 24.39, 6.9%
```

 6.9% of 16 x 1509.0 us over 90544 packets is 18 ns each, where 27 was taken. In long rows (e16) the same bytes took less:

```profile
q10 hardware_dynamic: 27568, 24.39, 5.2%
```

 The Trainium skill has transfers under 512 B below line rate ("DMA: Bandwidth & Descriptors", "Specifications"); 6.9% against 5.2% for the same 24.39 MB agrees. But no wait of TensorE was found that only the pieces explain.
- **Rival 1** was refuted by any of the five waits; **rival 4** by the pace.
- **The signs of being wrong** that I named didn't come: sets of 128 columns took 0.28 us, not 0.5, block transposes 0.42, not 0.7, and no group waited for the evictions of the one before. All three looked at the groups and none at the ends of the halves.
